# A norm product deferred into the next position step, and two residual loads moved ahead of the sixth transform

## The chip, the cores and the metric

The kernel runs on one core of a Trainium2 chip. The time is device microseconds of one execution. TensorE (PE in the profile) does the matrix products, VectorE (DVE) and ScalarE (ACT) the elementwise work, GpSimd (POOL) small products and some DMA issues, SyncE (SP) issues most of the DMAs. Every engine and every DMA-issuing queue works through its own instructions strictly in order; between engines there are only semaphores.

## The reference

A two-layer bidirectional encoder over 2048 prompt positions and 512 sample positions, 1024 channels, in float32. Layer 0 is windowed grouped-query attention, layer 1 is a Fourier mixer: the real part of a 2-D DFT over positions and over the 256 channels of each of 4 groups. Each branch is gated by SiLU, mapped by an output matrix and added to the residual. A final RMSNorm follows.

```
x = attention_layer(x, ...)
h = rmsnorm(x, g)
f = jnp.fft.fftn(hg, axes=(1, 3), norm="ortho").real
gate = h @ w_gate
x = x + (f * jax.nn.silu(gate)) @ w_out
y = rmsnorm(x, final_norm)
```

## The kernel before

Products in float32 are made of three products of split numbers: each operand is a high part (a cast on ACT) and a low part (a subtraction on DVE), and `matmul3` (L92 to L95) issues high x high, high x low, low x high. So an operand of a product costs an ACT cast and a DVE subtraction before TensorE can read it.

The change lies in the last part of the second layer, from L1588 on. The DFT over positions is split in two: sums of sixteen row groups (`pm`, additions and subtractions of 128x1024 tiles on DVE, L1598, recorded at L1184), and then for each `k1` from 0 to 8 a DFT over 128 positions, called a position here. A position is `position` (L1330 to L1367): in two halves of 512 channels it makes the split operands `gp` of its sums (`halves_of`, L1316: casts at L1323, subtractions at L1324), multiplies them with a cosine part into a bank `Ap` and a sine part into `Bp`, and joins the two into one or two row blocks `up` (L1354 to L1361). The sine parts of both halves lie in one PSUM bank, `Bp`, so the second half's sine products follow the last read of the first half's, which is the subtraction at L1361. At the end each `up` is multiplied by the stored gate `s2p` (L1364).

`step` (L1516) strings positions together. It runs the new positions, then `finish` (L1384) of the first of the two row blocks that the step before left in `pend`, then the transposes and splits of the new blocks (`split_T`, L960), then `finish` of the second. A `finish` loads the residual rows `x` from DRAM (`residual`, L1379, L1381), makes 48 products `fo` of the row block with the output matrix in two banks of 512 columns, adds each to `x` (L1392), and calls `normed` (L1373). That one is the final RMSNorm: a sum of squares on ACT (`jkf`, L982), a small scaling on DVE (`invf`, L88), a power on POOL (L89), the product of the whole 128x1024 row block with the norm on DVE (L1376), and the store to the output from SP (L1377).

The steps in order are the positions 0 and 8 (L1612), 4 (L1622), 2 (L1643), and then position 6 (L1657), which is written out: its operands are made early (`p6`, L1651), the stores of the sums of positions 7, 3 and 5 go to DRAM from the ACT queue (`god`, L1656), and after the transform come the loads of the operands `fT1` and `fT2` (`f_sums`, L1505), the two `finish` calls of position 2's blocks (rows 2 and 14), `Outs.operands` (transposes `tr` at L1409 and the splits and sums of them) and `Outs.load` (two more residual loads). From there on the output product uses seven products for eight (`Outs.products`, banks `Wo`, `Zo`, `Xo`). The banks `fo`, `Wo`, `Zo` and `Xo` come from one set of three PSUM buffers, tag `acc`.

Three things set the order of the work here.

- The instruction streams are not the order of the text. A planner orders each engine's stream at build time with its own durations: it takes, of what is ready by its count, what comes first in the text. So `pm` sums and `fo` products of later lines fill gaps of earlier ones. What it has ordered stays: an engine whose next instruction is not ready waits.
- `after(a, b)` (L135) holds an instruction behind another in its engine's stream, without a wait. The norm product at L1376 is held behind `last_b[0]`, the last L1361 that had been written when it was.
- Tiles of a tag share buffers, and a tile takes a buffer when all users of the tile before it are through; tiles of one tag take buffers in the order of the text. The tag `x` (L80) has four buffers of 512 KB. In this part they hold the gates `s2p` (for a mirrored block loaded by a gather that POOL issues, L1310; else from SP, L1307) and the residual rows `x`. A residual's buffer is free when its store to the output has landed; a gate's, when the product at L1364 has read it.

Of the kernel before, what the change touches and what calls it, by code (L numbers as in the profile page):

```python
# [14 lines left out]
ALU = mybir.AluOpType  # L15
# [22 lines left out]
def f32(ap):  # L38
    return ap.bitcast(F32)
# [3 lines left out]
def encoder(  # L43
# [3 lines left out]
    PE, ACT, DVE, POOL, SP = nc.tensor, nc.scalar, nc.vector, nc.gpsimd, nc.sync  # L47
# [87 lines left out]
    def after(ins, anchor):  # L135

        if anchor is not None:
            tc.add_manual_dep(ins.ins, anchor.ins.name, ISSUE, reason="issue order")
# [794 lines left out]
    def fourier_phase(tail):  # L933
        with ExitStack() as es:
# [356 lines left out]
            gfb = fp.tile([P, D], F32, tag="gb", bufs=1, name="gfb")  # L1291
# [21 lines left out]
            def position_loads(name, tab, tiles):  # L1313
                return [gated(name, r, xtile) for r in tiles], table(name, tab, left)

            def halves_of(name, gr, gs, hf):  # L1316

                out = []
                for i, g in enumerate((gr, gs)):
                    if g is not None:  # L1320
                        t = main.tile([P, 2, 512], F32R, align_bytes=LINE, tag="hT", bufs=8, name=f"g{name}_{hf}_{i}")
                        gv = g[:, hf * 512 : hf * 512 + 512]
                        ACT.copy(t[:, 0], gv)  # L1323
                        DVE.tensor_tensor(t[:, 1], gv, f32(t[:, 0]), ALU.subtract)  # L1324
                        out.append(t)
                return out

            last_b = [None]

            def position(name, tab, gr, gs, tiles, loads=None, parts=None, between=None, later=None):  # L1330

                s2s, tb = loads or position_loads(name, tab, tiles)
                cs, sn, ns = [(tb[:, 2 * i], tb[:, 2 * i + 1]) for i in range(3)]
                bp = bank(f"B{name}")
                us = [zt(f"u{name}_{i}") for i in range(len(tiles))]
                for hf in range(2):
                    if hf and between:
                        between()
                    ts = parts[hf] if parts and parts[hf] else halves_of(name, gr, gs, hf)

                    def acc(out, tabs, c0, n):
                        for i, (w, t) in enumerate(zip(tabs, ts)):
                            v = [
                                t[:, part].rearrange("p (g c) -> p g c", g=2)[:, :, c0 : c0 + n]
                                for part in range(2)
                            ]
                            matmul3(out, w, v, i == 0, i == len(ts) - 1)

                    a = bank(f"A{name}_{hf}")[:, :260].rearrange("p (g c) -> p g c", g=2)
                    acc(a, (cs, ns), 0, 130)  # L1350
                    b = bp[:, hf * 256 : hf * 256 + 256].rearrange("p (g c) -> p g c", g=2)
                    acc(b, (sn, cs), P, P)
                    uv = [u.rearrange("p (g c) -> p g c", g=4)[:, 2 * hf : 2 * hf + 2] for u in us]
                    ACT.copy(uv[0][:, :, 0 : P + 1], a[:, :, 0 : P + 1])  # L1354
                    re, im = uv[0][:, :, 1:P], b[:, :, 1:P]
                    for v in uv[1:]:
                        ACT.copy(v[:, :, 0 : P + 1 : P], a[:, :, 0 : P + 1 : P])
                        DVE.tensor_tensor(v[:, :, 1:P], re, im, ALU.add)
                        DVE.tensor_tensor(v[:, :, P + 1 : 256], re, im, ALU.subtract)
                    DVE.tensor_tensor(uv[0][:, :, P + 1 : 256], re, im, ALU.add)  # L1360
                    last_b[0] = DVE.tensor_tensor(re, re, im, ALU.subtract)  # L1361
                for u, s2 in zip(us, s2s):
                    if later is None:
                        DVE.tensor_tensor(u, u, s2, ALU.mult)  # L1364
                    else:
                        later.append(lambda u=u, s2=s2: after(DVE.tensor_tensor(u, u, s2, ALU.mult), last_c[0]))
                return list(zip(us, tiles))  # L1367

            def out_rows(r):
                dst, off = (y_prompt, 0) if r[0] < SEQ else (y_sample, SEQ)  # L1370
                return rows(dst, (r[0] - off, r[1]))

            def normed(x2, r):  # L1373

                inv = sumsq(x2, f"f{r[0]}")
                after(DVE.scalar_tensor_tensor(x2, x2, inv[:, 0:1], gfb, ALU.mult, ALU.mult), last_b[0])  # L1376
                SP.dma_start(out_rows(r), x2)  # L1377

            def residual(r):  # L1379
                x2 = x_tile(f"x2_{r[0]}")  # L1380
                SP.dma_start(x2, rows(x1d, r))  # L1381
                return x2

            def finish(uT, r):  # L1384
                r0 = r[0]
                x2 = residual(r)
                for half in range(2):
                    ps = psum2.tile([P, 512], F32, tag="acc", name=f"fo{r0}_{half}")
                    for k in range(KD):
                        matmul3(ps, uT[k], wo[half * KD + k], k == 0, k == KD - 1)  # L1390
                    xs = x2[:, half * 512 : half * 512 + 512]
                    DVE.tensor_tensor(xs, xs, ps, ALU.add)  # L1392
                normed(x2, r)

# [111 lines left out]
            def pair(k1, R, base):  # L1508

                if k1 == 0 or 2 * k1 == R:  # L1510
                    return [(base + k1, R, None)]
                return [(base + k1, R, None), (base + R - k1, R, k1 if R == 16 else 0)]

            pend = []

            def step(*positions):  # L1516
                new = [t for p in positions for t in position(*p)]
                if pend:
                    finish(*pend.pop(0))
                new = [(split_T(u, f"u{r[0]}", r[2] is not None), r) for u, r in new]  # L1520
                for f in pend:
                    finish(*f)
                pend[:] = new

            def sample(k1, ids, g_place, s2_places, tb_place):
# [62 lines left out]
            G = {}  # L1588
# [20 lines left out]
            f, g4s = pm(w0[1], w0[3], "f0")  # L1609
# [38 lines left out]
            g1r, g7r = pm(e0c, o0c, "g1r")  # L1648
            g1s, g7s = pm(o0s, e0s, "g1s")
            g3r, g5r = pm(e1c, o1s, "g3r")  # L1650
            p6 = [halves_of("p6", *G[6], hf) for hf in range(2)]  # L1651
            g5s, g3s = pm(o1c, e1s, "g5s")
            G[1], G[7], G[3], G[5] = (g1r, g1s), (g7r, g7s), (g3r, g3s), (g5r, g5s)
            for k1 in (7, 3, 5):
                for t, g in zip(god[k1], G[k1]):
                    ACT.dma_start(t, g)  # L1656
            o = Outs(6, position("p6", 6, *G[6], pair(6, 16, 0), None, p6))  # L1657
            f_sums("T1", right)
            f_sums("T2", right)
            finish(*pend.pop(0))  # L1660
            o.operands()
            finish(*pend.pop(0))
            o.load()

            def reads(k1):
# [135 lines left out]
```

## Time and profile before

| what | value |
|---|---|
| median of 3 runs | 1583.85 us (1583.34 to 1585.53) |
| the profiled execution | 1584.07 us, span 1582.1 us |
| PE busy | 1569.5 us (99%) |
| DVE busy | 1151.0 us (73%) |
| ACT busy | 874.5 us (55%) |
| POOL busy | 446.5 us (28%) |
| DMA | 373.89 MB, mean 236 GB/s |

Views of the profile used below: the stretches (busy time of each engine in a window, with the granted TensorE clock and the DMA share), the waits, and the timeline, in which neighbouring instructions of one group are merged; there a row has its start in us from the span's start, its length, the engine, the line, the operation, what is written from what, the count, and in brackets the idle time before it with its releaser. An engine name with a q is that of its queue, which issues a DMA. The rows of DMA issues give the size and the time from issue to landing.

### The profile page before, as it was taken

What the parts mean: (1) busy time and instruction counts of PE and PEld (TensorE: products, weight loads), DVE (VectorE), ACT (ScalarE), POOL (GpSimd) and SP (SyncE); (2) the same over time, 40 slices, a digit from 0 to 9 for tenths busy, and PEclk for the clock granted to TensorE, in tenths of its full rate; (3) what the DMA queues carried; (4) which work ended last, traced back from release to release, by engine and by line L of the source; (5) the groups of instructions that cost most, each with busy time, mean ns of one, the idle gap of its engine ahead of it and who ended that gap; (6) DMA issues with size and microseconds to landing.
All of it is one profiled execution on the core that took longest, in us unless ns stands there. A gap on an engine that the chain in (4) does not pass through costs nothing.

```text
span 1582.1 us, 27442 instructions
## 1 busy us (share of the span) xinstructions
PE 1569.5 (99%) x9743; PEld 1320.8 (83%) x9743; DVE 1151.0 (73%) x2785; ACT 874.5 (55%) x2089; POOL 446.5 (28%) x613
## 2 busy tenths in 40 slices
PE   9999999999999999999999999999999999999998
PEld 7888888888888888988888888888888888887886
DVE  6888656877447886378764577669778878988896
ACT  6688535776246784267752576646555554343342
POOL 2475642421404314024222242223112111011110
PEclk9999999999999999999999999999999999999999
DMA  7598695575856567655659566675567469548752
GB/s 293 200 332 290 227 359 210 207 262 201 295 205 224 205 234 276 216 215 214 257 165 329 208 221 232 236 262 196 196 207 258 175 223 410 183 167 318 264 203 80
DMA packets 101445, 373.89 MB, mean 236 GB/s; under 512 B 12236, under 2 KB 22476, under 8 KB 83901
## 3 DMA queue, kind: packets, MB, share of 16 engines
q1 hardware_dynamic: 82572, 297.91, 52.7%
q0 software_dynamic: 16400, 70.04, 11.4%
q10 hardware_dynamic: 2336, 4.20, 0.7%
q8 instruction: 77, 1.26, 0.3%
q14 instruction: 60, 0.48, 0.1%
HBM read 280.84 MB, written 91.26 MB: 235 GB/s over the span
## 4 chain that ended last, share of the span: by engine, by line
PE 95%; DVE 2%; DMA 1%; issue 0%; ACT 0%; POOL 0%; SPq 0%; DVEq 0%; POOLq 0%; ACTq 0%
PE gp L95 14%; PE qp L95 14%; PE spt L95 11%; PE op L95 7%; PE W L95 6%; PE av L557 6%; PE spt L472 6%; PE fo L95 5%; PE vp L95 3%; PE Z L95 3%; PE Wo L95 3%; PE pt L531 3%; PE Zo L95 2%; PE z L95 2%; PE X L95 2%; PE z L1079 1%
## 5 line engine op out<-in xcount | busy, mean ns | idle before, releaser
L95 PE MATMUL gp<-h,wg 128*128 128x512 f32 x960 | 237.6, 395 | 0.0
L95 PE MATMUL qp<-h,wq 128*128 128x512 f32 x960 | 237.3, 396 | 0.0
L491 DVE CUSTOM_DVE_ANT_0 S<-spt,b 128x385 f32<-128x385 f32 (+1 forms) x320 | 156.3, 527 | 105.1 <-PE spt L472 68.1
L95 PEld LDWEIGHTS gp<-h,wg 128*128 128x128 f32 x960 | 174.9, 188 | 37.2 <-issue 1.0
L95 PEld LDWEIGHTS qp<-h,wq 128*128 128x128 f32 x960 | 174.9, 188 | 36.7 <-issue 0.2
L499 ACT ACTIVATE S<-S 128x385 f32<-128x385 f32 (+1 forms) x320 | 188.8, 596 | 19.7 <-DVE S L491 19.5
L539 ACT CAST pts<-pt 128x384 fp32r<-128x384 f32 (+1 forms) x240 | 100.5, 457 | 168.2 <-PE pt L531 158.6
L540 DVE TENSOR_TENSOR pts<-pt,pts 128x384 fp32r<-128x384 f32 (+1 forms) x240 | 114.3, 519 | 23.3 <-ACT pts L539 22.2
L95 PE MATMUL spt<-wo,uT 128*128 128x512 f32 x480 | 120.4, 391 | 0.0
L581 POOL TENSOR_TENSOR uT<-o,uT 128x256 fp32r<-128x256 f32 x75 | 55.5, 739 | 229.3 <-ACT uT L580 229.2
L95 PE MATMUL op<-wo,uT 128*128 128x512 f32 x480 | 118.9, 391 | 0.0
L472 PE MATMUL spt<-kwin,qab 64*128 64x384 f32 (+1 forms) x960 | 118.4, 352 | 0.0
L557 PEld LDWEIGHTS av<-pts,v 128*128 128x128 f32 x576 | 101.4, 188 | 18.8
L95 PE MATMUL fo<-wo,tTu 128*128 128x512 f32 x480 | 115.7, 392 | 0.3 <-ACT wo L1556 0.3
L557 PE MATMUL av<-pts,v 128*128 128x512 f32 (+1 forms) x576 | 115.7, 341 | 0.0
L95 PEld LDWEIGHTS op<-wo,uT 128*128 128x128 f32 x480 | 89.3, 188 | 18.5
L95 PEld LDWEIGHTS spt<-wo,uT 128*128 128x128 f32 x480 | 89.1, 188 | 18.4
L95 PEld LDWEIGHTS fo<-wo,tTu 128*128 128x128 f32 x480 | 88.3, 188 | 17.6 <-ACT wo L1556 0.7
L511 DVE TENSOR_SCALAR S<-S 128x384 f32<-128x384 f32 (+1 forms) x192 | 96.0, 500 | 6.8
L472 PEld LDWEIGHTS spt<-kwin,qab 64*128 64x128 f32 x960 | 74.6, 186 | 28.2 <-issue 26.4
L577 POOL TENSOR_TENSOR o<-o,s 128x256 f32<-128x256 f32 x75 | 55.3, 737 | 135.1 <-DVE o L575 134.7
L531 PEld LDWEIGHTS pt<-ident,S 64*128 64x128 f32 x1328 | 78.4, 138 | 4.0 <-issue 1.8
(322 smaller groups left out, 3190.9 us busy)
## 6 DMA issues: line engine op xcount, KB each, us to landing
wo<-wsd SPq DMA_DIRECT2D x32, 1024.0 KB, 4.9
wq<-wsd SPq DMA_DIRECT2D x31, 1024.0 KB, 7.4
wg<-wsd SPq DMA_DIRECT2D x31, 1024.0 KB, 5.4
x<-x1d SPq DMA_DIRECT2D x40, 512.0 KB, 3.5
b<-b21d SPq DMA_DIRECT2D x40, 512.0 KB, 5.7
b<-rowd SPq DMA_DIRECT2D x40, 384.0 KB, 4.3
xs<-in_x_dram SPq DMA_DIRECT2D x23, 512.0 KB, 6.4
s2d<-gt POOLq DMA_DIRECT2D x40, 256.0 KB, 5.2
```

The costliest lines, as they stand in the source:

```text
L95: pe(PE.matmul(out, a[i], b[j], start=start and i + j == 0, stop=stop and i == 1, skip_group_check=more))
L472: pe(PE.matmul(banks[j][:, 2 + k0 * P : 2 + k1 * P], res["q"][rows, qp, b * P : (b + 1) * P], kwin[g][rows, kp, b * P + k0 * P : b * P + k ...
L491: seq(DVE, DVE.tensor_tensor_reduce(out=s[:, e0:e1], in0=ps[:, 1 + e0 : 1 + e1], in1=st["bias"][:, j, 386 - e1 : 386 - e0][:, ::-1], scale ...
L499: last_exp[0] = seq(ACT, ACT.activation(s[:, e0:e1], s[:, e0:e1], AF.Exp, bias=s[:, 386:387], scale=-1.0, accum_out=s[:, 387:388]))
L511: seq(DVE, DVE.tensor_scalar(s[:, ks], s[:, ks], den, None, ALU.mult))
L531: pe(PE.transpose(ps[h][:, kb, j, :], ss[j][rows, 1 + kb * P : 1 + (kb + 1) * P], ident[rows, rows]))
L539: seq(ACT, ACT.copy(hi, ps[:, k0:k1]))
L540: seq(DVE, DVE.tensor_tensor(lo, ps[:, k0:k1], f32(hi), ALU.subtract))
L557: pe(PE.matmul(to, v, pt, start=n == part == 0, stop=part == 1 and n in (1, len(todo) - 1), skip_group_check=n > 1,))
L577: eng.tensor_tensor(o, o, s, ALU.mult)
L581: low = eng.tensor_tensor(lo, o, f32(hi), ALU.subtract)
L1079: PE.matmul(to, m[part][:, g * P : (g + 1) * P], ch[:, 0, :, odd * P : (odd + 1) * P], start=part == 0, stop=part == 1,)
```

## The change

Three edits. First, `finish` and `normed` get a flag `wait`. With it, the sum of squares, the scaling and the power are written where they were, but the norm product and the output store are put into a list `due`. `position` empties that list behind the L1361 of a first half. `step` sets the flag for its second block, so that block's product and store come in the next position. Since `after` is called then, the product is held behind that first half's L1361.

Second, position 6 gets only the operands of its first half made early; those of its second half are made inside `position`, behind what `due` held.

Third, the two residual loads of the `finish` calls around position 6 are written ahead of `position("p6", ...)`, and so ahead of that position's gate loads, and handed to `finish`.

```
-            last_b = [None]
+            last_b, due = [None], []
...
                     last_b[0] = DVE.tensor_tensor(re, re, im, ALU.subtract)
+                    while due:
+                        due.pop()()
...
-            def normed(x2, r):
+            def normed(x2, r, wait=False):
 
                 inv = sumsq(x2, f"f{r[0]}")
-                after(DVE.scalar_tensor_tensor(x2, x2, inv[:, 0:1], gfb, ALU.mult, ALU.mult), last_b[0])
-                SP.dma_start(out_rows(r), x2)
+
+                def scale():
+                    after(DVE.scalar_tensor_tensor(x2, x2, inv[:, 0:1], gfb, ALU.mult, ALU.mult), last_b[0])
+                    SP.dma_start(out_rows(r), x2)
+
+                if wait:
+                    due.append(scale)
+                else:
+                    scale()
...
-            def finish(uT, r):
+            def finish(uT, r, wait=False, x2=None):
                 r0 = r[0]
-                x2 = residual(r)
+                x2 = x2 or residual(r)
...
-                normed(x2, r)
+                normed(x2, r, wait)
...
                 for f in pend:
-                    finish(*f)
+                    finish(*f, True)
...
-            p6 = [halves_of("p6", *G[6], hf) for hf in range(2)]
+            p6 = [halves_of("p6", *G[6], 0), None]
...
+            rest = [residual(r) for u, r in pend]
             o = Outs(6, position("p6", 6, *G[6], pair(6, 16, 0), None, p6))
             f_sums("T1", right)
             f_sums("T2", right)
-            finish(*pend.pop(0))
+            finish(*pend.pop(0), x2=rest[0])
             o.operands()
-            finish(*pend.pop(0))
+            finish(*pend.pop(0), x2=rest[1])
             o.load()
```

## The prediction

> **What bounds the kernel now.** I read the page's first part, then the stretches around the steps, then the waits of PE, then the timeline of the two places where PE waits. The page:
>
> ```profile
> span 1582.1 us, 27442 instructions
> PE 1569.5 (99%) x9743; PEld 1320.8 (83%) x9743; DVE 1151.0 (73%) x2785; ACT 874.5 (55%) x2089; POOL 446.5 (28%) x613
> ```
>
> TensorE is busy for all but 12.6 us. The stretches of the steps that the change touches (columns: window, its length, busy us of PE, PEld, DVE, ACT, POOL, granted clock, DMA share, GB/s):
>
> ```profile
> 1376.00:1403.00 27.00, 26.92 (x139) 22.68 (x138) 20.38 (x30) 13.17 (x22) 2.11 (x3) 1.00 0.57 211
> 1403.00:1430.00 27.00, 26.73 (x137) 22.46 (x136) 25.83 (x36) 7.29 (x16) 2.84 (x3) 1.00 0.34 117
> 1430.00:1460.00 30.00, 29.69 (x151) 24.97 (x150) 26.13 (x39) 10.49 (x21) 4.19 (x4) 1.00 0.89 337
> 1460.00:1490.00 30.00, 28.63 (x149) 24.09 (x148) 24.48 (x42) 11.63 (x24) 4.39 (x5) 1.00 0.89 329
> ```
>
> PE is idle for 0.08, 0.27, 0.31 and 1.37 us in them: 2.03 us, 0.13% of the time. No matmul is removed, so this is the most that the change can gain. The waits of PE name the last three:
>
> ```profile
> PE Zo L95 <- issue: 1.4, 1, 1.4
> PE Ap L95 <- DVE gp L1324: 0.3, 1, 0.3
> PE Bp L95 <- DVE up L1361: 0.3, 1, 0.3
> ```
>
> About 0.2%, 3.2 us, is what a measurement of this kernel can tell from no change. The ceiling lies under it; the question is what the change costs.
>
> **The change part by part.** Terms are made against the profiled execution (1584.07 us, 0.22 us over the median of the runs); the forecast is then put on the median. No instruction is added: three norm products, three stores, two loads and four splittings change place.
>
> *The product in positions 4 and 2.* Position 2, on DVE:
>
> ```profile
> 1406.37 0.41 DVE L1360 TENSOR_TENSOR up<-up,Bp 128x254 f32<-128x254 f32 x1
> 1407.18 1.28 DVE L1376 SCALAR_TENSOR_TENSOR x<-x,invf,gfb 128x1024 f32<-128x1024 f32 x1 [0.40 <-POOL invf L89]
> 1408.38 0.41 DVE L1361 TENSOR_TENSOR up<-up,Bp 128x254 f32<-128x254 f32 x1
> 1408.85 0.74 PE L95 MATMUL Bp<-gp,tbp 128*128 128x256 f32 x4 [0.27 <-DVE up L1361]
> ```
>
> The product stands between L1360 and L1361, and the second sine half waits for L1361. In the other order L1361 runs at 1406.7, in the 0.40 us in which DVE waits for POOL, and the product still starts when POOL delivers, at 1407.18. Its store leaves when it left. So 0.27 us goes, and 0.08 us in position 4, whose window is the first row of the stretches. Nothing is late next: the buffer comes free at the same time.
>
> *The product in position 6.* Here it moves far:
>
> ```profile
> 1435.65 1.28 DVE L1376 SCALAR_TENSOR_TENSOR x<-x,invf,gfb 128x1024 f32<-128x1024 f32 x1 [0.44 <-POOL invf L89]
> 1436.85 1.22 DVE L1184 TENSOR_TENSOR od<-od,od 128x1024 f32<-128x1024 f32 x1
> 1437.99 1.89 DVE L1324 TENSOR_TENSOR gp<-ev,gp 128x512 fp32r<-128x512 f32 x3
> ...
> 1443.65 0.41 DVE L1361 TENSOR_TENSOR up<-up,Bp 128x254 f32<-128x254 f32 x1
> ...
> 1446.69 1.22 DVE L1364 TENSOR_TENSOR up<-up,s2p 128x1024 f32<-128x1024 f32 x1
> ```
>
> ```profile
> 1444.71 0.88 PE L95 MATMUL Bp<-gp,tbp 128*128 128x256 f32 x6
> ```
>
> The wait and product took 1.64 us (0.44, and 1.20 from start to start), and two of the three L1324 at 0.60 each belong to the second half, which now comes later. The first half's splitting, for which PE waits 0.31 us, is done 1.64 us sooner: that 0.31 us goes. L1361 moves from 1443.65 to 1440.8, and the product ends at 1442.4 (0.33 + 1.28 after), against 1436.9 before.
>
> *The second half's splittings.* They follow at 1442.4, two at 0.60 us: ready at 1443.6. The second half's six sine products ran at 1444.71, and `fo` products are there to run meanwhile. Zero; without that cover, up to the 1.2 us.
>
> *The residual loads.* The 1.37 us is this:
>
> ```profile
> 1451.64 1.41 SPq L1381 DMA_DIRECT2D x<-x1d  x3
> ...
> 1461.11 1.28 DVE L1392 TENSOR_TENSOR x<-x,fo 128x512 f32<-128x512 f32 x2 [3.12 <-PE Wo L95]
> ...
> 1461.90 3.00 PE L95 MATMUL Zo<-fT,S 128*128 128x512 f32 x12 [1.37 <-issue]
> ```
>
> ```profile
> x<-x1d SPq DMA_DIRECT2D x1, 512.0 KB, 9.4
> ```
>
> The first of the three loads (rows 14) is issued at 1451.64 behind eight operand loads and lands 9.4 us on, at 1461.0. The addition that needs it starts at 1461.11 and frees the `acc` bank that `Zo` takes at 1461.90. The row says "issue" and "PE Wo", but both had long been done. Ahead of position 6 this load takes the buffer of a gate that position 2's L1364 has read before the gather at 1415 (its row is below): some 45 us early. The 1.37 us goes. The other load (rows 2) moves ahead as well; no engine that matters waited for it.
>
> *What pays for that.* Four buffers, taken in the order of the text. The two residuals now take the two that position 6's gates had. The gate of its first block moves to the buffer that the residual of rows 2 had; that residual was added long before L1364 at 1446.69, so the load is early enough there: zero. The mirrored gate moves to the buffer of the residual whose product was deferred, and its gather on POOL must wait for that store:
>
> ```profile
> 1415.06 1.73 POOL L1310 DMA_INDIRECT s2p<-s2d,mir  x1 [7.92 <-DVE up L1364]
> ```
>
> So a gather that was 31 us early joins a chain: product to 1442.4, store, gather, L1364, transposes. The rows that price it (the store first in quiet, at 1395.54, then in traffic, at 1451.25; then the gather issued at 1415, the one at 1450.77, and two between these, issued at 1483.63 and 1386.73):
>
> ```profile
> out_dram<-x SPq DMA_DIRECT2D x1, 512.0 KB, 2.6
> out_dram<-x SPq DMA_DIRECT2D x1, 512.0 KB, 8.4
> s2p<-s2d,mir POOLq DMA_INDIRECT x1, 4.8
> s2p<-s2d,mir POOLq DMA_INDIRECT x1, 9.2
> s2p<-s2d,mir POOLq DMA_INDIRECT x1, 6.4
> s2p<-s2d,mir POOLq DMA_INDIRECT x1, 8.5
> ```
>
> With 1.2 us for L1364 the transposes can start at 1442.4 + 2.6 + 4.8 + 1.2 = 1451.0 at the earliest, at 1442.4 + 8.4 + 9.2 + 1.2 = 1461.2 at the latest. They stood here:
>
> ```profile
> 1449.76 1.91 PE L1409 MATMUL tr<-ident,up 128*128 128x128 f32 x16
> 1451.42 6.38 PE L95 MATMUL fo<-wo,tTu 128*128 128x512 f32 x27
> 1457.64 2.88 PE L95 MATMUL Wo<-wo,tT 128*128 128x512 f32 x12
> ```
>
> ```profile
> 1453.10 0.69 DVE L957 TENSOR_TENSOR S<-F,S 128x512 fp32r<-128x512 f32 x1
> ```
>
> With 0.66 us gained before them their place is 1449.1, so they are 1.9 to 12.1 us late. I take 3.5 us for the store, near the quiet end: the operand loads that SP has ahead of it start sooner than before (they queued behind the old store), and the rest queue behind it. For the gather I take 7.4, the mean of 6.4 and 8.5, since that rest (0.89 DMA share in this stretch) runs beside it. That is 1454.5, 5.4 us late.
>
> Cover: 27 `fo` and 12 `Wo` products, about 9 us, need only the other block. But PE takes its stream as the planner laid it. It will put the transposes behind some `fo`, by its own durations; I suppose them those of quiet transfers, because its one error that PE felt here, the 1.37 us, was a load in traffic taken as too early. Then 1.9 us is covered and 3.5 us is a stall. Bounds: no stall, if it counts the traffic too, and 12.1 us, if the transposes stay and everything is slow. What hangs on the transposes, `Zo`, came 12.1 us after they began, and its operand S was split 4.0 us after they began (the L957 row); this slack covers it.
>
> A rule on the gather: the Trainium skill, "DMA: Bandwidth & Descriptors", section "Queues, rings and completion order", says that each DMA engine takes turns between the queues that have work, packet by packet. By that a gather, on POOL's own queue, would not stand behind SP's backlog but get every other turn: as an estimate 4.8 us and once more its transfer (1.3 us at about 400 GB/s), 6.1 us, a stall of 2.2 instead of 3.5 us. The 8.5 and 9.2 us rows are against it, and both stalls lie in the forecast case.
>
> *Queues.* On SP the deferred store, ready at 1442.4, holds the operand loads behind it by some 5 us; all of these were issued before 1451.64 and `fT2` is read at 1466.18, so even 9.4 us from 1456.6 ends as it is read, and a stall adds cover: zero, at most a few tenths.
>
> ```profile
> 1466.18 2.91 PE L95 MATMUL Wo<-fT,S 128*128 128x512 f32 x12
> ```
>
> On POOL the gather stands ahead of the next norm's power and a table load; if the store is slow they wait with it, and only an output store and the next position hang on them, over 10 us later.
>
> **Sum.** -0.08 - 0.27 - 0.31 - 1.37 + 3.5 = +1.5 us: 1585.6 on the profiled execution, 1585.3 on the median, +0.09%.
>
> **The rivals.**
>
> *Covered.* The planner sets the transposes far enough behind. For it: the order of before has 99% of PE busy, so its counts are mostly good, and 9 us of other products stand ready. Against it: the 1.37 us. It gives -2.03: 1581.8 us, no change by the bound.
>
> *The gather decides (slower).* Place: the mirrored block's transposes. It ends as slower when the stall passes 2.03 + 3.2 = 5.2 us, that is when the transposes can start 7.1 us late, at 1456.2; a store of 4.5 us and a gather of 8.5 do it, or 1454.3 if the planner leaves them in place. For it: 8.5 and 9.2 us are the two gathers with SP loads beside them. At a stall of 8 us the time is 1583.85 - 2.03 + 8 = 1589.8. In this rival a second price may come. After the last matmul the clock falls:
>
> ```profile
> 1577.00:1583.00 6.00, 0.00 (x0) 0.00 (x0) 1.42 (x2) 0.00 (x0) 0.26 (x1) 0.66 0.23 87
> ```
>
> 0.66 in the mean over 6 us, so half the clock from about 1579, 4 us after PE stopped; the 1.37 us gap left it at 1.00. The Trainium skill, "TensorE: Matmul & The Clock Gate", Part 1, says that PE is gated to half after about 3.4 us of idling and needs as long busy to come back; a stall beyond that would cost an estimated 1.7 us more, 1591.5; I give that a quarter of this rival's chance, since the row is from the end of the run, where PE does not come back.
>
> *The change does not do what it says.* The product is held by order only; if the planner lets L1361 wait anyway, or gives `acc` banks another order, 0.66 us stay. By itself it changes no sign: with the stall, 1586.0.
>
> **How the numbers follow.** Forecast case, a stall of 1 to 5.2 us, 1582.8 to 1587.0: 0.37. Covered: 0.23. Gather decides: 0.32. The change misses its aim: 0.04, counted as no change. A gain past 3.2 us is more than the idle time there is: 0.04 for what I don't see. So faster 0.04, within 0.64, slower 0.32. The likeliest is 1585.3; the range reaches from the covered case to the slower rival, 1581.6 to 1590.2.
>
> **What would show it.** Right: L1376 behind L1361 in positions 4 and 2 and no PE wait there; the residual of rows 14 loaded near 1415, and no wait before the first `Zo`; the gather on POOL issued after 1444; a PE wait of some 3 us before `tr`, released by L1364. Wrong: a gather still at 1415 (then the buffers go another way and the covered case holds), transposes that PE reaches after their data, or PE waits on `fT2`.

## The result and the profile after

The changed kernel takes 1594.38 us (median of six runs, 1590.96 to 1595.42) against 1583.85 us before: ratio 1.006, 95% interval 1.005 to 1.007. It is slower by some 10 us, outside the predicted range (1581.6 to 1590.2 us). The profiled execution took 1592.06 us, 7.99 us more than that of before. Lines after the edits are shifted: the norm product L1376 is now L1380, the addition L1392 is L1401, the gate product L1364 is L1366, the transposes L1409 are L1418, the residual load L1381 is L1390.

The page of after begins with:

```profile
span 1590.2 us, 27442 instructions
PE 1573.6 (99%) x9743; PEld 1322.7 (83%) x9743; DVE 1150.1 (72%) x2785; ACT 874.8 (55%) x2089; POOL 450.4 (28%) x613
```

The same stretches as before, and the one behind them (window, length, busy us of PE, PEld, DVE, ACT, POOL, granted clock, DMA share, GB/s), and then the waits of PE in this part:

```profile
1376.00:1403.00 27.00, 27.00 (x140) 23.07 (x139) 20.83 (x30) 13.17 (x22) 2.43 (x3) 1.00 0.55 210
1403.00:1430.00 27.00, 27.00 (x141) 22.91 (x140) 26.31 (x37) 7.40 (x17) 1.10 (x2) 1.00 0.32 117
1430.00:1460.00 30.00, 24.80 (x121) 20.25 (x121) 19.76 (x29) 4.29 (x10) 9.21 (x5) 0.96 0.88 319
1460.00:1490.00 30.00, 29.80 (x147) 25.34 (x147) 24.44 (x41) 12.92 (x26) 3.31 (x4) 0.92 0.78 288
1490.00:1520.00 30.00, 28.49 (x141) 23.20 (x140) 24.98 (x43) 14.22 (x29) 4.05 (x4) 1.00 0.55 188
```

```profile
PE tr L1418 <- DVE up L1366: 5.2, 1, 5.2
PE Ap L95 <- ACT gp L1323: 1.5, 2, 0.8
PE tr L1418 <- ACT jkf L982: 0.2, 1, 0.2
```

All the waits that the change aimed at are gone: PE is busy for the whole of the first two stretches, and no wait on L1361, on L1324 or before the first `Zo` is left. In their place stands one wait of 5.2 us before the second set of transposes in position 6, and two at the operands of position 7. The timeline shows how the first comes about:

```profile
1443.07 0.69 DVE L1401 TENSOR_TENSOR x<-x,fo 128x512 f32<-128x512 f32 x1 [1.93 <-PE fo L95]
1443.67 0.41 DVE L1361 TENSOR_TENSOR up<-up,Bp 128x254 f32<-128x254 f32 x1
1444.00 1.28 DVE L1380 SCALAR_TENSOR_TENSOR x<-x,invf,gfb 128x1024 f32<-128x1024 f32 x1
1447.10 1.29 DVE L1380 SCALAR_TENSOR_TENSOR x<-x,invf,gfb 128x1024 f32<-128x1024 f32 x1 [0.34 <-POOL invf L89]
1448.30 1.22 DVE L1366 TENSOR_TENSOR up<-up,s2p 128x1024 f32<-128x1024 f32 x1
1449.79 0.99 POOL L1310 DMA_INDIRECT s2p<-s2d,mir  x1 [2.73 <-DVE up L1366]
1450.05 4.59 PE L95 MATMUL fo<-wo,tTu 128*128 128x512 f32 x19
1458.46 1.22 DVE L1366 TENSOR_TENSOR up<-up,s2p 128x1024 f32<-128x1024 f32 x1 [6.82 <-DMA s2p<-s2d,mir]
1459.83 2.79 PE L1418 MATMUL tr<-ident,up 128*128 128x128 f32 x12 [5.20 <-DVE up L1366]
```

The store of rows 12 (issued at 1445.31) and the gather, from issue to landing:

```profile
out_dram<-x SPq DMA_DIRECT2D x1, 512.0 KB, 2.9
s2p<-s2d,mir POOLq DMA_INDIRECT x1, 8.6
```

The gather of position 6's mirrored gate, at 1415 before, is now issued at 1449.79. What released it is not the store, which landed at 1448.2, but L1366 of the direct block (the row at 1448.30). That product comes 1.6 us later than before (1446.69), because the norm product of rows 2 (the row at 1447.10), which is not deferred, was laid ahead of it and waits 0.34 us for POOL. The profile does not show buffers; in the built program the gather's tile takes the buffer that position 6's own direct gate had, which L1366 leaves at 1449.5. It lands 8.6 us later; PE had 19 `fo` products (to 1454.6) and then nothing until 1459.83. After that the clock is low:

```profile
1454.00:1460.00 6.00, 0.80 (x4) 0.39 (x3) 1.22 (x1) 0.00 (x0) 0.00 (x0) 0.81 1.02 344
1460.00:1466.00 6.00, 6.00 (x24) 5.26 (x24) 4.10 (x7) 3.65 (x7) 0.00 (x0) 0.62 1.01 392
1466.00:1472.00 6.00, 6.00 (x32) 5.11 (x31) 5.43 (x10) 4.00 (x8) 0.87 (x1) 1.00 0.45 180
```

In narrower windows of this trace the clock is 1.00 up to 1457.7, 0.50 from 1457.8 to 1464.5 and 1.00 again from 1464.6. So it is either whole or half here, and the time at half is twice the part that is missing: 2 x (0.19 x 6 + 0.38 x 6) = 6.8 us. PE was idle in the first 2.1 of these; in the other 4.8 it lost half, 2.4 us.

The account of the profiled executions: -2.03 (the idle time of before) + 5.2 + 0.2 + 1.5 (waits) + 2.4 (clock) = +7.3 of the 7.99 us. The rest, 0.7 us, has no row of its own.

### The profile page after: what moved, and what is told of

Its sections match the earlier page's. It is cut to its first block, busy times and chain, and to the rows that moved or that the text cites. A ratio compares the mean times of both kernels' runs of the same rounds, so it can differ in the third digit from the quotient of the medians.

```text
span 1590.2 us, 27442 instructions
## 1 busy us (share of the span) xinstructions
PE 1573.6 (99%) x9743; PEld 1322.7 (83%) x9743; DVE 1150.1 (72%) x2785; ACT 874.8 (55%) x2089; POOL 450.4 (28%) x613
```

## The experiments

Each time stands beside that of the kernel before in the same rounds (1583.57 to 1584.47 us); ratios are to it, with 95% intervals.

### One half of the change at a time

The deferral without the early loads:

```
-            rest = [residual(r) for u, r in pend]
-            finish(*pend.pop(0), x2=rest[0])
+            finish(*pend.pop(0))
```

> The deferral alone: products and stores of second row blocks come in the next position, the second half's operands of position 6 are made late, but the two residual loads stay where they were before. Theory (the mirrored gate's gather takes a buffer late because the two loads are ahead of it): the gates of position 6 keep early buffers, the gather is issued near 1415, PE does not wait before the transposes; the 0.66 us of the waits on L1361 and on the splitting are gained, the 1.4 us wait before the first Zo stays, give or take 1.5 us: 1583.2 us, 1582 to 1585. Rival A (the deferred product and its store, which hold the operand loads on SP, cost the time): the loss stays, 1590 us or more.

Measured: 1585.69 us, 1.0005 (0.9996 to 1.0014): no change that can be told, though a little above the expected range. The gather is issued at 1414.39 and PE has no wait before position 6's transposes. So the deferral alone does not make the changed kernel slow, and rival A falls; but the 0.66 us was not to be seen either: the profile has two waits that the kernel before had not, 0.8 us at a `Wo` product and 0.6 us at position 7's operands.

The early loads without the deferral:

```
+            rest = [residual(r) for u, r in pend]
             o = Outs(6, position("p6", 6, *G[6], pair(6, 16, 0), None, p6))
-            finish(*pend.pop(0))
+            finish(*pend.pop(0), x2=rest[0])
```

> The two loads alone: the kernel before, with the residual loads of rows 2 and 14 written ahead of position 6. Theory: the mirrored gate takes the buffer that the residual of rows 12 leaves, so the gather is issued when the store of rows 12 has landed. The norm product ends at 1436.9 as before; store 3 us, gather 8.6 us and L1364 1.2 us give 1449.7, where the transposes stood (1449.76). So little or no stall with the store and gather as quick as in the changed kernel, up to 6 us with the slow rows (8.4 and 9.2 us); the 1.4 us wait before the first Zo goes. 1583 us, 1582.3 to 1588. Rival A (the deferral costs the time): 1582.3 us, without any late gather. Rival B (the early loads cost it by their traffic or their buffers, whatever the deferral does): 1590 us or more.

Measured: 1587.27 us, 1.0016 (1.0007 to 1.0025). PE waits before the transposes (the waits of PE):

```profile
PE tr L1409 <- DVE up L1364: 3.3, 1, 3.3
```

and the clock falls to half for 2 x (0.08 x 6 + 0.21 x 6) = 3.5 us (stretches of the same run):

```profile
1448.00:1454.00 6.00, 2.66 (x13) 1.95 (x12) 2.88 (x5) 0.00 (x0) 1.56 (x2) 0.92 1.02 415
1454.00:1460.00 6.00, 6.00 (x31) 5.44 (x30) 5.36 (x8) 3.69 (x7) 1.77 (x2) 0.79 1.04 386
```

Here the gather takes the buffer of rows 12's residual, as I had thought it would in the changed kernel; it is issued at 1441.01 and takes 9.5 us. So the early loads alone make the gather late, and cost 2.8 us; with the deferral it is 8.8 us later still. Neither half alone gives the 9 to 10 us.

### The gate's buffer

The mirrored gate in a buffer of another set:

```
-            o = Outs(6, position("p6", 6, *G[6], pair(6, 16, 0), None, p6))
+            t6 = pair(6, 16, 0)
+            l6 = [gated("p6", r, place) for r, place in zip(t6, (xtile, left))], table("p6", 6, left)
+            o = Outs(6, position("p6", 6, *G[6], t6, l6, p6))
```

> The changed kernel, but the mirrored gate of position 6 lies in a buffer of the set left, as those of the later positions do, so its gather waits for no buffer of the tag x. Everything else is as changed: deferral, late second half, loads ahead. Theory: gather issued before 1430, no wait of PE before the transposes, no half clock, and the 1.5 us of waits at position 7's operands go with the stall: 1583.85 - 2.03 = 1581.8 us, 1581 to 1583. Rival A (the late product and its store): 1590 us or more, since both stay. Rival C (the waits in position 7 and the slower rows after it come from the loads' order and not from the stall): 1584 to 1586 us.

Measured: 1587.22 us, 1.0017 (1.0007 to 1.0026). The wait of 5.2 us is gone and 1430 to 1460 is full (30.00 of 30.00), so most of the loss was the gate's buffer. But 2.8 us are left, where I expected a gain of 2. Its waits of PE are further on, and two rows of its timeline ahead of them are of interest:

```profile
PE Ap L95 <- ACT gp L1323: 2.7, 2, 2.1
PE tr L1418 <- ACT jkf L982: 1.3, 1, 1.3
```

```profile
1469.15 0.69 DVE L1466 TENSOR_TENSOR x<-x,Zo 128x512 f32<-128x512 f32 x1 [1.81 <-PE Zo L95]
1469.76 0.41 DVE L1361 TENSOR_TENSOR up<-up,Bp 128x254 f32<-128x254 f32 x1
```

The transposes of position 1 come 1.3 us late (the row names ACT; L1366 ended at the same time, 1476.5), the loads of position 7's operands `go` follow them, and after the wait for these loads the clock is at 0.50 for some 6.8 us. The timeline rows show an order on DVE that comes back below: the subtraction L1361 of position 1 stands behind an addition that waits 1.81 us for PE. So there is a second cause, and no theory had the size.

Which queue fills the late buffer, by writing the mirrored gate first:

```
+            m6 = gated("p6", t6[1], xtile)
+            l6 = [gated("p6", t6[0], xtile), m6], table("p6", 6, left)
```

> The changed kernel, but position 6's mirrored gate is written ahead of the direct one, so the gather takes the early buffer and SP's direct load (L1307) the late one, when the mirrored block's L1366 has read its gate. Theory (the late buffer costs the time, whichever queue fills it): the gather is issued near 1415, SP's load after 1446, and PE waits before the first transposes, by 2 to 6 us: 1588 to 1595 us. Rival (the gather on POOL is what is slow): no wait before the transposes, 1587 us or less, as with the gate in the other set.

Measured: 1585.58 us, 1.0012 (1.0003 to 1.0021), and no wait before position 6's transposes: the expectation was wrong. SP's load, from issue to landing:

```profile
s2p<-s2d SPq DMA_DIRECT2D x1, 512.0 KB, 4.1
```

It is issued at 1446.54, 3.2 us before the gather of the changed kernel, ahead of the `fT2` loads, and takes 4.1 instead of 8.6 us. It can be issued sooner because the gate product that frees the buffer runs at 1445.29, ahead of the norm product of rows 2, and not at 1448.30. So a late buffer alone does not make the stall. Three things differ here at once, the time of the issue, the place in SP's order, and a plain load in place of a gather; this run does not tell them apart.

The traffic, by moving the four `fT2` loads:

```
             f_sums("T1", right)
-            f_sums("T2", right)
             finish(*pend.pop(0), x2=rest[0])
             o.operands()
+            f_sums("T2", right)
```

> The changed kernel with the four fT2 loads written behind position 6's transposes, so SP issues them after the gather of the mirrored gate and not in the 3 us before it. The gather is still late. Theory (the gather shares the DMA engines with what SP has issued just before it): it takes 5 to 6.5 us instead of 8.6, the stall before the transposes is 2 to 3.5 us instead of 5.2. Rival (by turns between the queues the backlog of SP does not matter): the gather takes 8 us or more as before, the stall stays at about 5. The whole time says less, since fT2 may come late at its own products: 1588 to 1596 us.

Measured: 1591.54 us, 1.0041 (1.0027 to 1.0054). The gather from issue to landing, and then the stretch of the stall:

```profile
s2p<-s2d,mir POOLq DMA_INDIRECT x1, 6.0
```

```profile
1454.00:1460.00 6.00, 3.47 (x23) 2.79 (x22) 2.00 (x3) 1.17 (x3) 0.00 (x0) 1.00 0.97 314
```

With little of SP's ahead of it the gather takes 6.0 instead of 8.6 us, the wait before the transposes is 2.5 instead of 5.2 us, and the clock stays at 1.00 behind it. What SP has issued just before does slow a gather on another queue. The time is lost again in later waits (1.6 and 2.5 us) and in 3.4 us at half clock from 1494.5 on.

More cover, by holding the transposes behind the rest of `fo` and all of `Wo`:

```
+                        between()
+                        prod(self.W, self.A[0, 0], wo[0:4], range(4), True)
+                        hold = last_mm[0]
-                    self.turn(1, 0)
+                    self.turn(1, 0, hold)
```

> The changed kernel, but the transposes of position 6's mirrored block are held behind the last three fo products and the twelve Wo products, which need only what is ready. The gather is as late as in the changed kernel. PE reaches the transposes at 1454.6 + 0.7 + 2.9 = 1458.2 instead of 1454.6, so the wait for L1366 is 1.5 us instead of 5.2; a second wait of some 2 us then comes before the first Zo, for the split of S, with the transposes (1.4 us at full clock) between the two. Theory on the clock (it falls only after more than about 3 us without products): it stays at 1.00, Zo starts 3.7 us sooner, 1594.4 - 3.7 = 1590.7 us, 1589.5 to 1592. Rival (the clock goes by the share of idle time and falls anyway): 1593 us or more. Rival on the cover (the planner's order hid nothing that could have helped): 1594 us.

Measured: 1589.28 us, 1.0035 (1.0021 to 1.0048), just below the expected range. The waits of PE, and the stretch behind the longer one:

```profile
PE Zo L95 <- ACT S L955: 3.7, 1, 3.7
PE tr L1418 <- DVE up L1366: 1.5, 1, 1.5
```

```profile
1464.00:1470.00 6.00, 5.60 (x16) 4.17 (x17) 6.00 (x11) 5.16 (x10) 0.00 (x0) 0.72 0.94 299
```

The first wait is 1.5 us as expected, the second 3.7 instead of 2, with 2 x 0.28 x 6 = 3.4 us at half clock behind it. So cover was there, and it was worth 3.7 us (5.5 us over before instead of 9.2); but what the transposes feed waits in turn.

### The late second half

Both halves' operands made early again, with the gate moved, and then with the gate left in its place:

```
-            p6 = [halves_of("p6", *G[6], 0), None]
+            p6 = [halves_of("p6", *G[6], hf) for hf in range(2)]
```

> The changed kernel with the mirrored gate in the set left and with both halves of position 6's operands made early, as before; the product is still deferred. SP's order from the store of rows 14 on is as in the run with the gate alone moved: the store of rows 6 stands ahead of the go loads. Theory (SP's order): the waits at position 7 stay, 1585.5 to 1588 us. Rival (the late second half is what costs): the waits go, 1582 us, up to 1583.5.

Measured: 1582.94 us, 0.9992 (0.9983 to 1.0001). The rival was right and my theory on SP's order wrong: 1.8 + 0.4 us of waits at position 7 remain, but the 1.3 us before the transposes and the half clock are gone.

> The changed kernel with both halves of position 6's operands made early, as before; the mirrored gate stays in a buffer of the tag x. With the runs on the gate's set this makes a square of four: gate late and halves late 1594.4, gate alone moved 1587.2, both 1582.9 us. The first half's L1361 runs some 3 us sooner (1440.3 instead of 1443.7), so the gate product that frees the buffer ends some 3 us sooner, and the gather of 8 to 10 us is still in the chain to the transposes. Theory (two causes that add): the stall before the transposes stays, at 2 to 5 us with its half clock, and the loss of the late halves, 4.3 us, goes: 1588 to 1591 us. Rival (the late halves alone delay the gather, and without them it comes in time): 1582 to 1584 us. Rival (the gather alone counts): 1593 us or more.

Measured: 1589.09 us, 1.0029 (1.0017 to 1.0042), with a wait of 4.0 us before the transposes (5.2 us as changed) and none before those of position 1. The run changes more than the half: in this built program the gather's tile has the buffer of rows 12's residual, as the prediction had it, and not that of the direct gate. The gather is issued at 1446.15, behind the store of those rows (issued at 1442.34, 3.0 us to landing).

The changed kernel itself in a later set of rounds:

> The changed kernel itself once more, on the chip and in the rounds of the two runs beside it. Expected from its first runs: 1594.4 us, 1591 to 1595.5; the stall of 5.2 us and the half clock behind it in the profile.

Measured: 1592.96 us, 1.0059 (1.0046 to 1.0073), a wait of 5.1 us. Over the kernel before, the four are: as changed +9.2 us, gate moved +2.8, halves early +4.6, both -0.9. The gate's buffer is worth 5.5 to 6.4 us and the late second half 3.7 to 4.6 us (from the first measurement of the changed kernel, 10.5 us over before, the upper figures would be 1.3 us higher). Two causes, and they nearly add. Two limits: where the gate stays in its set, making both halves early also moves the gather to another buffer, so that row of the square does not show the half alone; and the late half is not always this dear, for the deferral alone, which has it too, was only 1.2 us over before, and that within the noise.

Through what does the late half cost? First SP's order at the `go` loads:

```
-                    SP.dma_start(out_rows(r), x2)
+                    after(SP.dma_start(out_rows(r), x2), last_go[0] if r[0] == 6 else None)
```

> The changed kernel with the mirrored gate in the set left, and one thing more: SP's store of rows 6 is held behind the four go loads of position 7, as it stood in the kernel before. TensorE's stream is the same, row for row. In the run without this, SP issued that store at 1479.18 and the go loads from 1479.62 on, and PE waited 2.11 and 0.63 us for the casts of go, after which the clock stood at 0.50 for 6 to 7 us. Theory (SP's order is the second cause): the go loads are issued about 1.2 us sooner, as the transposes free their buffers; the 2.11 us wait falls under 1.2 us and the clock stays at 1.00: 1587.2 - 1.2 - 3 = 1583 us, 1582 to 1584.5. Rival (the loads are slow because of the gather and the x loads beside them, whatever their place): nothing changes, 1586.5 to 1587.5.

Measured: 1585.32 us, 1.0008 (0.9999 to 1.0017); without this edit 1.0017 (1.0007 to 1.0026). The intervals overlap; the waits at position 7 fall from 2.7 to 1.8 us. A small part at most. With both halves early the same edit gives nothing:

> The changed kernel with three things undone or moved: gate in the set left, both halves early, and SP's store of rows 6 behind the go loads of position 7. In the run without the last, PE waits 1.8 + 0.4 us at position 7's first products. Theory: the go loads are issued about 0.5 us sooner, the gather of the next gate beside them (9.6 us) still slows them: 1582 us, 1581 to 1583. If SP's order is the main cause of those waits: 1580.8 us.

Measured: 1583.74 us, 0.9995 (0.9986 to 1.0004), a little above the expected range too.

Then the order on DVE. In the changed kernel the addition at 1443.07 waits 1.93 us for PE with L1361 behind it. Held behind L1361, without and with the gate moved:

```
-                    DVE.tensor_tensor(xs, xs, ps, ALU.add)
+                    add = DVE.tensor_tensor(xs, xs, ps, ALU.add)
+                    if r0 == 2 and half:
+                        after(add, first_b[0])
```

> The changed kernel with one order changed on DVE: the addition of rows 2 to its second bank (L1401), which waited for the bank until 1443.07, is held behind the first half's L1361, which stood behind it and ran at 1443.67. Theory (the late second half costs because that addition comes ahead of L1361): L1361 runs at 1441.1, the norm product ends at 1442.7 instead of 1445.3, the gather is issued 2 to 3 us sooner, the stall before the transposes falls from 5.2 us to 2 to 3.5 us, and with it some of the half clock: 1588 to 1591 us, as with both halves early (1589.1). Rival (the late halves cost elsewhere, in the splittings themselves or later): 1593 us or more.

Measured: 1591.38 us, 1.0047 (1.0034 to 1.0061). From the timeline, and from the waits of PE (L1422 and L1368 are L1418 and L1366 there):

```profile
1441.14 0.42 DVE L1361 TENSOR_TENSOR up<-up,Bp 128x254 f32<-128x254 f32 x1
```

```profile
PE tr L1422 <- DVE up L1368: 2.3, 1, 2.3
PE Ap L95 <- ACT gp L1323: 2.8, 2, 2.1
```

L1361 runs 2.5 us sooner and the wait falls to 2.3 us, as expected, but the waits at position 7 grow from 1.5 to 2.8 us and 1.3 us come before position 1's transposes; only 1.6 us are gained against the changed kernel beside it. The gather goes another way here, too:

```profile
1446.44 0.99 POOL L1310 DMA_INDIRECT s2p<-s2d,mir  x1 [6.52 <-DVE x L1403]
1446.77 1.23 DVE L1368 TENSOR_TENSOR up<-up,s2p 128x1024 f32<-128x1024 f32 x1
```

It is issued before the direct block's gate product begins, so it can't have waited for that. In this built program its tile has the buffer of rows 12's residual, whose store landed at 1445.7; the gather follows that by 0.8 us, as it does in the run with the loads alone (1440.2 and 1441.01). The addition that the row names ended at the same time. This is the chain of the prediction, and near its terms: product to 1442.8 (1442.4 forecast), store 2.9 us (3.5), stall 2.3 us (3.5). The time is still 7.6 us over before. What makes it up, as an estimate, is -2.03 + 2.3 + 2.8 + 1.3 us of waits and some 3.1 us for two spells of 3.4 us at half clock, from 1456.55 and from 1494.10, in which PE was idle for 0.6 us only: 7.5 us. So most of the loss lies behind the forecast stall, not in it.

> The same order on DVE in the kernel whose mirrored gate lies in the set left (1587.2 us without it, 1582.9 with both halves early). Theory: the same 2.5 us sooner, so the row blocks of position 6 and what follows them are in time: 1583 to 1585 us. Rival (the late halves cost elsewhere): 1586.5 to 1588 us, unchanged.

Measured: 1587.34 us, 1.0023 (1.0012 to 1.0033): unchanged. This order in position 6 sets when the gather starts, but it is not what the late half costs otherwise. Left is position 1, where the rows of 1469.15 and 1469.76 above show the same pattern, an addition that waits for PE ahead of L1361:

```
-                    add(xa, 1, Z)
+                    after(add(xa, 1, Z), first_b["p1"] if self.n == 6 else None)
+                    hold[0] = p1_b[0] if self.n == 6 else None
                     prod(X, A[0, 1], wo[4:8], four, True)
```

> The changed kernel with the mirrored gate in the set left (1587.2 us), and the order of position 1 as it comes out with both halves early: on DVE the addition of Zo to rows 6 (L1466), which waited for PE until 1469.15 and had the first half's L1361 of position 1 behind it at 1469.76, is held behind that L1361; on PE the Xo and the last Wo products of position 6 are held behind position 1's second sine half. The late second half of position 6 stays. Theory (the late half costs because the planner then puts that addition ahead of L1361): L1361 runs at 1467.3, the sine half at 1469 instead of 1471.2, the 1.33 us wait before position 1's transposes goes, the go loads are issued 2 us sooner and the waits for them fall from 2.7 us to about 1 with the clock at 1.00: 1583 to 1584.5 us. Rival (the late half costs through something else in those 30 us): 1586.5 us or more.

Measured: 1584.60 us, 1.0002 (0.9993 to 1.0011); with the gate moved alone it was 1.0017. L1361 now follows L1360 at once, the wait before position 1's transposes is gone, and the clock stays at 1.00 from 1430 to 1520. The waits of PE that are left:

```profile
PE Ap L95 <- DVE gp L1324: 1.8, 1, 1.8
PE Ap L95 <- ACT gp L1323: 0.6, 1, 0.6
```

Over before it is 1.0 us instead of 2.8: 1.8 of the 3.7 us that the late half costs here, with intervals that touch (1.0007 to 1.0026 and 0.9993 to 1.0011). So about half of it comes through the order that the planner lays in position 1; DVE's and PE's order were changed together, and their shares are not told apart. The rest stays open.

### The loads where they cost nothing

The two loads behind position 6 and ahead of the operand loads, without any deferral, and with the deferral in positions 4 and 2 alone:

```
             o = Outs(6, position("p6", 6, *G[6], pair(6, 16, 0), None, p6))
+            rest = [residual(r) for u, r in pend]
             f_sums("T1", right)
```

> The kernel before, with one edit: the two residual loads are written behind position 6 but ahead of the eight operand loads; no product is deferred. Theory: the 1.37 us before the first Zo goes, the waits on L1361 and on the splitting (0.66 us) stay: 1583.8 - 1.4 = 1582.4 us. If the load order is worth more than the wait it removes, as the 2.6 us of the run that also defers in positions 4 and 2 may mean: 1581 to 1582 us.

Measured: 1582.66 us, 0.9988 (0.9979 to 0.9997).

> The deferral in positions 4 and 2 alone (not in position 6, whose operands are all made early as before), and the two residual loads written behind position 6 but ahead of the eight operand loads of f_sums. So position 6's gates keep their early buffers, and the load of rows 14 takes the buffer of the residual of rows 12, free at about 1440. Theory: 0.08 + 0.27 us of waits on L1361 and the 1.37 us before the first Zo go, the 0.31 us on the splitting stays: 1583.85 - 1.72 = 1582.1 us, 1581.5 to 1583. If the operand loads, now behind a load, come late: 1584 to 1586 us, with a wait of PE at the first Zo or at the Wo that reads fT2.

Measured: 1581.42 us, 0.9982 (0.9973 to 0.9991), and in the stretch that had the 1.37 us:

```profile
1460.00:1490.00 30.00, 30.00 (x158) 25.65 (x157) 23.97 (x41) 12.05 (x25) 4.93 (x5) 1.00 0.92 340
```

This version is faster than both kernels. The load still gets its buffer 11 us earlier than before (issued at 1440.41), and position 6's gates keep theirs.

## Why the prediction was wrong, step by step

Three steps failed: the place of the deferred product in position 6, and with it the buffer; the zero for the second half; and the nothing that the forecast's sum has behind the stall. The stall itself, 5.2 us, would give 1584.07 - 2.03 + 5.2 = 1587.2 us, inside the range. The other 4.8 us of the profiled execution are 1.7 us of later waits, 2.4 us of clock and 0.7 us without a row.

- **The ceiling and the four waits** (-0.08 -0.27 -0.31 -1.37): right. All four are gone in the profile after, and the two loads alone, put elsewhere, give 0.9988.
- **The product in position 6 ends at 1442.4**: wrong by 2.9 us (1444.00 + 1.28). I moved L1361 by what went from ahead of it; the planner put an addition there that waits 1.93 us for PE. This is the first failed step. With that order mended the product ends at 1442.8, the gather takes the buffer that I had named, and the stall is 2.3 us instead of 5.2.
- **The second half's splittings, zero**: wrong; this is the second failed step. It costs 3.7 to 4.6 us. Yet the half was not late where I looked: its splittings run at 1437.13 and 1438.87, not behind 1442.4, its first cosine products at 1438.11 (1439.54 before), and its sine products at 1444.22 (1444.71 before). About half of the cost, with the gate moved, lies 25 us later, in an order that the planner lays anew; the rest is open.
- **What pays**: the mechanism was right, the gather behind the deferred work. The buffer was not: it was not that of the deferred residual but that of position 6's own direct gate, so the gather waited for L1366 (free at 1449.5) and not for the store (landed at 1448.2). In the two runs in which the deferred product came in time (the addition held; both halves early) the buffer is the one that I had named. The terms: store 2.9 us against 3.5 taken, gather 8.6 against 7.4, issue at 1449.8 against 1445.9.
- **Cover**: 1.9 us was named, the planner laid 19 products, 4.6 us. So the transposes, 10.7 us later than their place of 1449.1, met a wait of 5.2 us, the very bound of the forecast case. Holding the transposes showed that more cover was there.
- **The rule of turns between queues** (the Trainium skill, "DMA: Bandwidth & Descriptors", section "Queues, rings and completion order"; 6.1 us for the gather, by my estimate from it): the runs disagree with the estimate, 8.6 us with SP's loads just ahead and 6.0 us without most of them, one gather each. The backlog of another queue counts for more than I took from the rule; whether the turns themselves are otherwise, no run here shows.
- **The clock's price**: right in kind. The rule of the Trainium skill, "TensorE: Matmul & The Clock Gate", Part 1, gave an estimated 1.7 us; the profile shows 2.4, and 1.7 in the second profile of the changed kernel. But I let it come only behind stalls beyond 3.4 us and gave it a quarter of one rival; the runs have it behind stalls from 1.8 us on, though not behind every one (the last section).
- **Queues, zero**: right for `fT2`, which is not waited for. Wrong for position 7's `go` loads, issued at 1486.93 against 1478.54 before and waited for by 1.5 us; I had stopped following SP at the operand loads.
- **The chances**: the rival "the gather decides", at 0.32, is nearest to what happened. That its 1591.5 us is near the measured time is luck in part: it has a stall of 8 us and 1.7 us of clock, where the profile has 5.2 us, 2.4 us of clock and 1.7 us of waits that it did not count.

Open: the 0.7 us of the account, and why most runs of the changed kernel lie above the profiled one. In the second profile the same wait was followed by 3.4 us at half clock instead of 6.8 (down at 1459.89, up at 1463.30), so one such stall has more than one price; that this makes the spread is not shown.

## What to carry to other kernels

A load moved ahead of others that share its buffers pushes one of them back: follow the chain of buffers to the last tile that now waits, and price that tile's transfer with the traffic of the place where it lands, not with that of the place it left. Where a planner lays the order, an operand whose making is written later can change the order of other engines a whole step further on; a cost of zero needs the cover there too. And a stall on TensorE of some 2 us or more is to be counted with one or two spells of 3.4 us at half clock behind it, which come or not by where the stall falls.

## What the runs showed of the clock

The time at half clock comes in pieces of one length. By twice the missing share it was 6.8 us (changed kernel), 3.5 (loads alone) and 3.4 (transposes held), and in the run with both halves early 2 x (0.13 x 6 + 0.44 x 6) = 6.8 us. That run's stretches:

```profile
1450.00:1456.00 6.00, 2.00 (x10) 1.45 (x9) 1.23 (x2) 0.00 (x0) 0.26 (x1) 0.87 1.04 367
1456.00:1462.00 6.00, 6.00 (x22) 5.20 (x21) 4.48 (x8) 4.03 (x8) 0.00 (x0) 0.56 0.86 336
```

Stretches laid on the steps of the clock show what it goes by. First the run with the `go` loads ahead, with the row of PE in which its wait ends, and then the run with the `fT2` loads moved:

```profile
1489.60:1493.02 3.42, 1.64 (x12) 1.34 (x12) 1.53 (x3) 1.78 (x4) 0.87 (x1) 1.00 0.47 127
1493.02:1496.43 3.41, 3.41 (x11) 2.74 (x10) 3.41 (x8) 0.17 (x1) 0.00 (x0) 0.50 0.45 185
```

```profile
1491.84 0.51 PE L95 MATMUL Ap<-gp,tbp 128*128 128x260 f32 x2 [1.78 <-DVE gp L1324]
```

```profile
1453.57:1456.98 3.41, 1.80 (x8) 1.15 (x7) 0.45 (x1) 0.00 (x0) 0.00 (x0) 1.00 1.02 348
1456.98:1460.40 3.42, 2.50 (x18) 2.32 (x19) 1.96 (x3) 1.57 (x3) 0.00 (x0) 1.00 0.89 279
```

In the first, an idle time of 1.78 us lies in one stretch of 3.4 us, and the whole of the next stretch is at half clock; the clock falls 1.2 us after PE has begun again. In the second, an idle time of 2.5 us lies across two stretches, 1.61 us in one and 0.92 us in the next, and the clock stays whole. The stretches are not chosen at will: wherever a trace has more than one step of the clock, the steps lie whole multiples of 3.413 us apart (in the changed kernel down at 1457.77, up at 1464.59 and, when the products are over, down at 1587.47, which is 2 and 36 of them). So the clock goes by the idle time within each stretch of a fixed rhythm, and not by the length of a gap alone.

How much idle time it takes can be read from the 18 traces. A stretch at whole clock with up to 1.68 us of idle time was never followed by half clock, one with 1.92 us or more always was, and the five from 1.70 to 1.91 us went both ways (the ends of products are modelled in the profile, so the border is no sharper than that). A stretch at half clock was followed by whole clock where PE was idle for up to 0.57 us in it, and by half clock again at 0.63, 0.96 and 2.07 us: the last three are the spells of 6.8 us. So the one wait of 5.1 to 5.2 us had two prices. In the first profile of the changed kernel the clock fell 2.1 us before PE began again, and that stretch was itself idle for 2.07 us, so a second followed; in the second profile the clock fell just as PE began again.

The Trainium skill, "TensorE: Matmul & The Clock Gate", Part 1, states a free-running window of 3.413 us; the steps here agree with it. It also says that the clock falls after an idle window; here a window with about half of it idle was enough.
